# Two-layer hybrid of four token mixers on one core: the scheduler's priority of weight splits and of the instructions that empty projection banks raised in the mixer stage

## The chip, the cores and the metric

The kernel runs on one core of one Trainium2 chip. The metric is device time in microseconds (us) of one execution. The core has a matmul engine, TensorE (PE in the profile; its weight loads are PEld), ScalarE (ACT), VectorE (DVE), GpSimd (POOL) and SyncE (SP), which here only issues transfers. PE runs at one of two clock levels, 1.2 or 2.4 GHz; the profile gives the granted clock as a share of 2.4 GHz.

## The reference, cut to what matters

256 tokens of width 1024 pass through two layers. In each, one in-projection feeds four mixers of 256 columns (hgrn2, gla, rwkv7, retention), an output projection and a layer norm follow, and then a feed-forward block: dense in layer 0, eight experts with two chosen per token in layer 1.

```python
for l in range(DEPTH):
    p = jnp.einsum('btd,dc->btc', h, w_in[l]).astype(F32)
    pa, pb, pc, pd = _split(p, MIXER_COLS)
    ya = _hgrn2_mixer(pa, lb_all[l], hgrn_norm_g[l])
    yb = _gla_mixer(pb, gla_gate_w2[l], gla_gate_b[l], gla_norm_g[l])
    yc, v_first = _rwkv7_mixer(pc, v_first, v_mix, ...)
    yd = _retnet_mixer(pd, positions, log_gamma)
    mix = jnp.einsum('btc,cd->btd', jnp.concatenate([ya, yb, yc, yd], axis=-1), w_out[l])
    h = _layer_norm(DN_ALPHA * h + mix, ln1_g[l], ln1_b[l])
    f = _swiglu(...) if l % 2 == 0 else _moe(...)
    h = _layer_norm(DN_ALPHA * h + f, ln2_g[l], ln2_b[l])
```

## The kernel before, in words

Every large product is computed to nearly f32 accuracy from two reduced-precision halves of each operand: `mm3` issues three matmuls per 128-row block of the contraction, high by high, high by low, low by high. The activations are split once per layer (tile XT). Weights are streamed: `load` has SP fetch a block of 256 columns (1 MB) into one of three `raw` buffers, and `pieces` splits it in three pieces of 3, 3 and 2 row blocks: ACT copies a piece to the high half (tile wH, `self.act`, L133), DVE subtracts that from raw for the low half (wL, `self.tt`, L136). There are three wH and three wL buffers. What `pieces` issues stands in `with self.tc.high_priority(self.hp)`; `self.hp` is HP in the mixers and 0 elsewhere. HP is a number by which an instruction counts as that much earlier in the program when the scheduler picks, engine by engine, the next instruction to write down. The order so written is what each engine runs, in that order.

The in-projection of a layer has fifteen full groups of 256 columns, 48 matmuls each, and a narrow one of 24: 744 matmuls. Each full group fills two PSUM banks, `Pws_ps` (weights stationary) or `Pas_ps` (activations stationary), out of a pool `acc` of three. A bank is free for the next group when its result has been read out: for rwkv by `rwkv_columns` (ACT writes rc_sh, DVE rc_x from bank and rc_sh), for queries, keys and values by `put` (ACT, tiles p_q, p_v), for gates by `silu2` (ACT then DVE, p_g), for gla's q and k by `gla_qk`, for hgrn's forget gate by `hgrn_gate` (DVE).

`mixers` runs rwkv first and then retention, hgrn and gla (ORDER = "rhg"). A mixer is a long chain of small steps that goes back and forth between PE, ACT, DVE and POOL. The groups for the later mixers are jobs: `between(n)` puts steps of them between the steps of the running mixer, so PE has in-projection matmuls to run while a chain is on the other engines. They are called fill here. When the fill of a layer is used up, the first blocks of the output projection (`out_proj`, tiles bank_acc and bank_r, 100 matmuls of 512 columns) serve instead: 52 of them (four that add alpha times h, and 48 for the rwkv and retention rows of w_out) need nothing of hgrn and gla; the last 48 wait for those two mixers' results. Their weights are split by the same `pieces`.

Names that come up: rw_rn (norm of rwkv's keys), rw_E (its decays), rw_kk, rw_ka (its keys), rw_AR and rw_BK (operands of its chunk products Prw_pss), rw_OC (its output), rt_o (retention's output), hg_E and Phs_p1p (hgrn's decays and scores), Pga, gs_lfH and gs_lfL, gs_E, Pgs, Ppo (gla's gate, the halves of its log decays, its decays, scores and output), hn_s and hn_rs (the norm of a mixer's output), y_late and Ppy (a mixer's result and its transpose, which feeds the output projection).

```python
            with self.tc.high_priority(self.hp):
...
                    self.split(H, L, raw[:, k0:k0 + m, :], eng)
```

Of the kernel before, what the change touches and what calls it, by code (L numbers as in the profile page):

```python
# [13 lines left out]
AF = mybir.ActivationFunctionType  # L14
OP = mybir.AluOpType
# [4 lines left out]
T = 256  # L20
# [19 lines left out]

ORDER = "rhg"

HP, OUTK = 60, (6, 4, 0, 2)

TAIL, DT = 4, 4

# [78 lines left out]
class Build:  # L125
# [156 lines left out]
    def ws(self, w, parts, ms=(128, 128), first=False):  # L282
        g = self.ws_steps(w, parts, ms, first)
        while True:
            try:
                next(g)
            except StopIteration as x:
                return x.value
# [339 lines left out]
    def mixers(self, l):  # L628
        nc, I, c, p = self.nc, self.I, self.c, self.otp
        W = I["w_in"][l]  # L630
        self.mp, self.side, self.hp = self.rp, "r", HP
        ws = lambda c0: self.ws_steps(W, [(c0, c0 + 256)])
        as_ = lambda c0: self.as_steps(W, [(c0, c0 + 256)])
        self.jobs = []

        def proj(kind):
            return p.tile([128, 2, 256], F32, name="p_" + kind, bufs=PB.get(kind, 1))

        def put(kind, ps, **k):
            dst = proj(kind)  # L640
            for i, x in enumerate(ps):
                self.act(dst[:, i, :], x, **k)
            return dst

        def silu2(kind, ps):

            dst = proj(kind)
            for i, x in enumerate(ps):
                self.act(dst[:, i, :], x, AF.Tanh, scale=0.5)
                self.stt(dst[:, i, :], dst[:, i, :], 1.0, x, OP.add, OP.mult)  # L650
            return dst
        def gla_qk(ps):
            gqk = proj("q")
            self.act(gqk[:, 0, :], ps[0], scale=float(32 ** -0.5))
            self.act(gqk[:, 1, :], ps[1])
            return gqk[:, 0:1, :], gqk[:, 1:2, :]
        q_, v_, g_ = (lambda ps: put("q", ps)), (lambda ps: put("v", ps)), (lambda ps: silu2("g", ps))
        J = {"h": lambda: [self.job(as_(256), lambda ps: self.hgrn_gate(ps)), self.job(ws(0), lambda ps: silu2("q", ps)),
                           self.job(as_(512), v_), self.job(as_(768), g_)],
             "g": lambda: [self.job(ws(O_GLA), gla_qk), self.job(as_(O_GLA + 256), v_), self.job(as_(O_GLA + 528), g_)],  # L660
             "r": lambda: [self.job(ws(O_RET), q_), self.job(ws(O_RET + 256), q_), self.job(as_(O_RET + 512), v_), self.job(as_(O_RET + 768), g_)]}
        J = {k: J[k]() for k in ORDER}
        glr = p.tile([128, T], F32, name="glr")
        nc.vector.memset(glr[32:64, :], 1.0)
        self.rwkv(l, glr)
        self.mp, self.side = self.otp, "o"
        steps = {"h": lambda f, q, v, g: self.hgrn(l, f, q, v, g),
                 "g": lambda qk, v, g: self.gla(l, glr, qk, v, g),
                 "r": lambda q, k, v, g: self.retnet(l, lambda i: (q, k)[i](), v, g)}
        for k in ORDER:  # L670
            steps[k](*J[k])

    def hgrn_gate(self, px):
        xf = self.otp.tile([128, 2, 256], F32, name="hg_xf")
        for tt, x in enumerate(px):
            self.ts(xf[:, tt, :], x, -44.0, None, OP.max)
        return xf

    def hgrn(self, l, xf, qT, V, G):  # L680
# [273 lines left out]
    def rwkv_columns(self, l, ci, glr):  # L954

        nc, W = self.nc, self.I["w_in"][l]
        c0 = O_RWKV + 256 * ci
        if ci < 4:
            ps, m = self.ws(W, [(c0, c0 + 256)], first=l == 0 and ci == 3), 128
        else:  # L960
            ps, m = self.ws(W, [(c0, c0 + 32), (O_GLA + 512, O_GLA + 528)], (48,)), 32
            nc.vector.tensor_copy(glr[32:48, :], ps[0][32:48, :])
        if ci == 3:
            self.layer_params(l)
        mu = self.pc["mu"]
        n = len(ps)

        sh = self.t2([128, 2, T], n="rc_sh")
        nc.gpsimd.memset(sh[:, :, 0:1], 0.0)
        x = self.t2([128, 2, T], n="rc_x")  # L970
        for j in range(n):
            g = 2 * ci + j
            self.act(sh[0:m, j, 1:T], ps[j][0:m, 0:T - 1], scale=mu[0:m, g:g + 1])
            self.stt(x[0:m, j, :], ps[j][0:m, :], self.om[0:m, g:g + 1], sh[0:m, j, :], OP.mult, OP.add)
        return x

    def rwkv(self, l, glr):
# [706 lines left out]
```

## Time and profile before

| | us |
|---|---|
| median of 3 runs | 1094.89 |
| lowest and highest of them | 1093.45 and 1101.36 |
| profiled execution | 1099.03 |
| its span, first to last instruction | 1097.2 |

The profiled execution is 4.14 us above the median; durations come from it. Times in the rows count from the start of its span. The mixers of layer 0 run to about 213 us, output projection and norm to about 232, the dense block to about 412; the mixers of layer 1 run from about 430 to 633, and the experts from about 660 to the end. In a timeline row stand start, length, engine, line, operation, output <- inputs, operand sizes and count; the bracket gives how long the engine had been idle and what released it. A matmul row's length reaches past the start of the next, since matmuls are pipelined; the distance of starts is what one costs.

### The profile page before, as it was taken

What the parts mean: (1) busy time and instruction counts of PE and PEld (TensorE: products, weight loads), DVE (VectorE), ACT (ScalarE), POOL (GpSimd) and SP (SyncE); (2) the same over time, 40 slices, a digit from 0 to 9 for tenths busy, and PEclk for the clock granted to TensorE, in tenths of its full rate; (3) what the DMA queues carried; (4) which work ended last, traced back from release to release, by engine and by line L of the source; (5) the groups of instructions that cost most, each with busy time, mean ns of one, the idle gap of its engine ahead of it and who ended that gap; (6) DMA issues with size and microseconds to landing.
All of it is one profiled execution on the core that took longest, in us unless ns stands there. A gap on an engine that the chain in (4) does not pass through costs nothing. (4 is left out here: it accounts for less than half of the span.)

```text
span 1097.2 us, 16969 instructions
## 1 busy us (share of the span) xinstructions
PE 1040.8 (95%) x6635; PEld 905.2 (83%) x6635; DVE 789.8 (72%) x1174; ACT 616.8 (56%) x872; POOL 60.5 (6%) x89
## 2 busy tenths in 40 slices
PE   7799989999999999899989989999999999999994
PEld 6788878789999788788877668888888888878883
DVE  4585674565556356675675578998999899989986
ACT  4634264435555342633264536787788678777862
POOL 2000021100000002000011210000000000010001
PEclk9899987999999999899988998999999999999997
DMA  9344144326666454244142095998899889979942
GB/s 299 99 119 128 57 154 155 116 78 192 193 192 228 157 192 156 87 115 131 65 164 78 12 366 191 359 381 302 313 348 362 307 306 364 357 269 328 365 179 80
DMA packets 142161, 228.83 MB, mean 209 GB/s; under 512 B 17604, under 2 KB 89848, under 8 KB 142072
## 3 DMA queue, kind: packets, MB, share of 16 engines
q1 hardware_dynamic: 135104, 219.76, 59.0%
q10 hardware_dynamic: 6968, 7.90, 2.2%
q8 instruction: 54, 0.88, 0.3%
q14 instruction: 35, 0.29, 0.1%
HBM read 224.50 MB, written 3.15 MB: 207 GB/s over the span
## 5 line engine op out<-in xcount | busy, mean ns | idle before, releaser
L136 DVE TENSOR_TENSOR wL<-raw,wH 128x1024 fp32r<-128x1024 f32 (+2 forms) x480 | 504.1, 1064 | 159.2 <-ACT wH L133 152.3
L133 ACT ACTIVATE wH<-raw 128x1024 fp32r<-128x1024 f32 (+2 forms) x481 | 441.9, 927 | 271.0 <-PE Pws_ps L146 95.8
L146 PE MATMUL Pws_ps<-XT,wH 128*128 128x256 f32 (+1 forms) x1248 | 233.2, 287 | 9.1 <-DVE rc_x L143 8.3
L146 PE MATMUL Pms_ps<-wH,e_X 128*128 128x512 f32 (+1 forms) x768 | 227.3, 374 | 0.0
L146 PEld LDWEIGHTS Pws_ps<-XT,wH 128*128 128x128 f32 (+1 forms) x1248 | 195.7, 191 | 12.8 <-DVE rc_x L143 9.2
L146 PE MATMUL Pws_ps<-XT,wL 128*128 128x256 f32 (+1 forms) x624 | 177.9, 286 | 0.0
L146 PEld LDWEIGHTS Pms_ps<-wH,e_X 128*128 128x128 f32 x768 | 142.3, 188 | 20.8
L146 PE MATMUL Pms_ps<-wL,e_X 128*128 128x512 f32 (+1 forms) x384 | 144.7, 377 | 1.0 <-DVE wL L136 1.0
L146 PEld LDWEIGHTS Pws_ps<-XT,wL 128*128 128x128 f32 (+1 forms) x624 | 119.3, 191 | 0.8 <-issue 0.3
L146 PE MATMUL bank_dn<-wH,e_aT 128*128 128x512 f32 x352 | 112.3, 396 | 0.6 <-DVE e_X L136 0.6
L146 PE MATMUL Pas_ps<-wH,XT 128*128 128x256 f32 x448 | 97.3, 305 | 4.6 <-ACT p_v L133 3.2
L146 PEld LDWEIGHTS Pas_ps<-wH,XT 128*128 128x128 f32 x448 | 76.8, 203 | 10.2 <-ACT p_v L133 4.5
L146 PEld LDWEIGHTS Pms_ps<-wL,e_X 128*128 128x128 f32 x384 | 72.2, 188 | 12.7 <-DVE wL L136 2.3
L146 PEld LDWEIGHTS bank_dn<-wH,e_aT 128*128 128x128 f32 x352 | 66.0, 188 | 16.7 <-DVE e_X L136 1.7
L146 PE MATMUL bank_dn<-wL,e_aT 128*128 128x512 f32 x176 | 69.4, 395 | 0.0
L146 PE MATMUL Pas_ps<-wL,XT 128*128 128x256 f32 x224 | 68.2, 305 | 0.5 <-DVE wL L136 0.5
L146 PEld LDWEIGHTS Pas_ps<-wL,XT 128*128 128x128 f32 x224 | 45.4, 203 | 3.1 <-DVE wL L136 1.8
L146 PEld LDWEIGHTS bank_dn<-wL,e_aT 128*128 128x128 f32 x176 | 33.1, 188 | 7.4
L146 PE MATMUL bank_acc<-wH,ffn_a 128*128 128x512 f32 x88 | 33.5, 394 | 0.0
L146 PE MATMUL bank_r<-wH,ffn_a 128*128 128x512 f32 x88 | 33.3, 392 | 0.0
L146 PE MATMUL bank_acc<-wH,YT 128*128 128x512 f32 x64 | 24.5, 416 | 1.2 <-ACT YT L133 1.2
L133 ACT ACT_TABLE_LOAD x19 | 24.4, 1283 | 1.6 <-PEq L1671 1.2
(386 smaller groups left out, 1223.8 us busy)
## 6 DMA issues: line engine op xcount, KB each, us to landing
raw<-in_moe_w_down SPq DMA_DIRECT2D x40, 1024.0 KB
raw<-in_moe_w_gate SPq DMA_DIRECT2D x32, 1024.0 KB
raw<-in_moe_w_up SPq DMA_DIRECT2D x32, 1024.0 KB
raw<-in_w_in SPq DMA_DIRECT2D x29, 1024.0 KB
raw<-in_moe_w_gate SPq DMA_DIRECT2D x16, 768.0 KB
raw<-in_moe_w_up SPq DMA_DIRECT2D x16, 768.0 KB
raw<-in_ffn_w_gate SPq DMA_DIRECT2D x11, 1024.0 KB
raw<-in_ffn_w_up SPq DMA_DIRECT2D x11, 1024.0 KB
```

The source lines that it names most:

```text
L133: return self.nc.scalar.activation(out=out, in_=in_, func=func, **k)
L136: return (eng or self.nc.vector).tensor_tensor(out=out, in0=a, in1=b, op=op)
L146: return self.nc.tensor.matmul(out=out, lhsT=lhsT, rhs=rhs, start=start, stop=stop)
```

## The change

HP goes from 60 to 400, so that the splits of streamed weights in the mixer stage count as 400 places earlier instead of 60. And five places that empty the banks of the in-projections, `put`, `silu2`, `gla_qk`, `hgrn_gate` and the loop of `rwkv_columns`, are put under the same priority, where they had none. No instruction is added or removed and none changes its operands. What changes is the order in which ACT, DVE, PE and SP run theirs; POOL's order is the same.

```diff
@@ -40,7 +40,7 @@
-HP, OUTK = 60, (6, 4, 0, 2)
+HP, OUTK = 400, (6, 4, 0, 2)
@@ -638,21 +638,24 @@
         def put(kind, ps, **k):
             dst = proj(kind)
-            for i, x in enumerate(ps):
-                self.act(dst[:, i, :], x, **k)
+            with self.tc.high_priority(HP):
+                for i, x in enumerate(ps):
+                    self.act(dst[:, i, :], x, **k)
             return dst
...
         def silu2(kind, ps):
             dst = proj(kind)
-            for i, x in enumerate(ps):
-                self.act(dst[:, i, :], x, AF.Tanh, scale=0.5)
-                self.stt(dst[:, i, :], dst[:, i, :], 1.0, x, OP.add, OP.mult)
+            with self.tc.high_priority(HP):
+                for i, x in enumerate(ps):
+                    self.act(dst[:, i, :], x, AF.Tanh, scale=0.5)
+                    self.stt(dst[:, i, :], dst[:, i, :], 1.0, x, OP.add, OP.mult)
             return dst
         def gla_qk(ps):
             gqk = proj("q")
-            self.act(gqk[:, 0, :], ps[0], scale=float(32 ** -0.5))
-            self.act(gqk[:, 1, :], ps[1])
+            with self.tc.high_priority(HP):
+                self.act(gqk[:, 0, :], ps[0], scale=float(32 ** -0.5))
+                self.act(gqk[:, 1, :], ps[1])
             return gqk[:, 0:1, :], gqk[:, 1:2, :]
@@ -673,8 +676,9 @@
     def hgrn_gate(self, px):
         xf = self.otp.tile([128, 2, 256], F32, name="hg_xf")
-        for tt, x in enumerate(px):
-            self.ts(xf[:, tt, :], x, -44.0, None, OP.max)
+        with self.tc.high_priority(HP):
+            for tt, x in enumerate(px):
+                self.ts(xf[:, tt, :], x, -44.0, None, OP.max)
         return xf
@@ -968,10 +972,11 @@
         x = self.t2([128, 2, T], n="rc_x")
-        for j in range(n):
-            g = 2 * ci + j
-            self.act(sh[0:m, j, 1:T], ps[j][0:m, 0:T - 1], scale=mu[0:m, g:g + 1])
-            self.stt(x[0:m, j, :], ps[j][0:m, :], self.om[0:m, g:g + 1], sh[0:m, j, :], OP.mult, OP.add)
+        with self.tc.high_priority(HP):
+            for j in range(n):
+                g = 2 * ci + j
+                self.act(sh[0:m, j, 1:T], ps[j][0:m, 0:T - 1], scale=mu[0:m, g:g + 1])
+                self.stt(x[0:m, j, :], ps[j][0:m, :], self.om[0:m, g:g + 1], sh[0:m, j, :], OP.mult, OP.add)
         return x
```

What that does to the order shows in three places. The first is ACT in layer 0, at the end of rwkv's key norm, where the two banks Pws_ps_416 and 417 (rwkv's receptance, read by rc_sh) and 495 and 496 (retention's queries, read by p_q) are to be emptied. Before:

```order
L133 ACTIVATE rw_rn<-rw_rn 128x512
L133 ACT_TABLE_LOAD
L133 ACTIVATE rw_rn<-rw_rn,rw_b_381 128x512
L133 ACTIVATE rw_E<-Prw_ps_393 128x2x256
L133 ACTIVATE rw_E<-Prw_ps_393 128x256
L133 ACTIVATE rw_E<-Prw_ps_400 128x2x256
L133 ACTIVATE rw_E<-Prw_ps_400 128x256
L133 ACTIVATE rc_sh<-Pws_ps_416,pcol 128x255
L133 ACTIVATE rw_A<-rw_A,psmall 128x256 x2
L133 ACTIVATE rw_AR<-rw_AR 64x8x64
L133 ACTIVATE rw_BK<-rw_BK 64x8x64
```

After:

```order
L133 ACTIVATE rw_rn<-rw_rn 128x512
L133 ACTIVATE p_q<-Pws_ps_495 128x256
L133 ACT_TABLE_LOAD
L133 ACTIVATE rw_rn<-rw_rn,rw_b_381 128x512
L133 ACTIVATE rw_E<-Prw_ps_393 128x2x256
L133 ACTIVATE rw_E<-Prw_ps_393 128x256
L133 ACTIVATE wH<-raw 128x768
L133 ACTIVATE rc_sh<-Pws_ps_416,pcol 128x255
L133 ACTIVATE rc_sh<-Pws_ps_417,pcol 128x255
```

The eviction of bank 495 has moved from behind everything shown to a place ahead of the table load, rc_sh ahead of half of rw_E, and a split stands between.

The second is DVE at the same place, where rc_x is the last reader of bank 416. Before:

```order
L143 SCALAR_TENSOR_TENSOR rw_kk<-rc_x,psmall,rw_rn 128x256 x2
L143 SCALAR_TENSOR_TENSOR rw_ka<-rw_A,rw_kk 128x512
L136 TENSOR_TENSOR rw_AR<-rw_kk,rw_E 128x8x64
L143 SCALAR_TENSOR_TENSOR rw_BK<-rw_ka,rw_E 128x8x64
L143 SCALAR_TENSOR_TENSOR rc_x<-Pws_ps_416,psmall,rc_sh 128x256
L136 TENSOR_TENSOR rc_x<-rc_x,rw_A 128x512
```

After:

```order
L143 SCALAR_TENSOR_TENSOR rw_kk<-rc_x,psmall,rw_rn 128x256 x2
L143 SCALAR_TENSOR_TENSOR rw_ka<-rw_A,rw_kk 128x512
L136 TENSOR_TENSOR wL<-raw,wH 128x768
L143 SCALAR_TENSOR_TENSOR rc_x<-Pws_ps_416,psmall,rc_sh 128x256
L143 SCALAR_TENSOR_TENSOR rc_x<-Pws_ps_417,psmall,rc_sh 128x256
L136 TENSOR_TENSOR wL<-raw,wH 128x768
L136 TENSOR_TENSOR wL<-raw,wH 128x512
L136 TENSOR_TENSOR rc_x<-rc_x,rw_A 128x512
```

rc_x no longer stands behind rw_AR and rw_BK, which feed rwkv's chunk products, but behind a split's low half; rw_AR and rw_BK come after two more splits.

The third is PE in layer 1, at gla's scores (Pgs) with output-projection matmuls (bank_acc, bank_r) among them. Before:

```order
L146 MATMUL bank_r<-wH,YT 128x512
L146 MATMUL bank_acc<-wH,YT 128x512
L146 MATMUL bank_acc<-wL,YT 128x512
L146 MATMUL Pgs_ps_6222<-gs_E 128x256
L146 MATMUL Pgs_ps_6222<-gs_E 128x128
L146 MATMUL Pgs_ps_6233<-gs_E 128x256
L146 MATMUL Pgs_ps_6233<-gs_E 128x128
L146 MATMUL Pgs_ps_6244<-gs_E 128x256
L146 MATMUL Pgs_ps_6244<-gs_E 128x128
L146 MATMUL bank_acc<-wH,YT 128x512
L146 MATMUL bank_r<-wH,YT 128x512
L146 MATMUL bank_r<-wL,YT 128x512
```

After:

```order
L146 MATMUL bank_r<-wL,YT 128x512
L146 MATMUL bank_r<-wH,YT 128x512
L146 MATMUL Pgs_ps_6205<-c_hlR,gs_lfH 128x128
L146 MATMUL Pgs_ps_6205<-c_hlR,gs_lfL 128x128
L146 MATMUL Pgs_ps_6205<-c_hlR,gs_lfH 128x128
L146 MATMUL Pgs_ps_6205<-c_hlR,gs_lfL 128x128
L146 MATMUL Pgs_ps_6222<-gs_E 128x256
L146 MATMUL Pgs_ps_6222<-gs_E 128x128
L146 MATMUL Pgs_ps_6233<-gs_E 128x256
```

Before, the matmul groups of the output projection stand up to Pgs_ps_6222 and between it and Pgs_ps_6259; now all of those that need nothing of hgrn and gla are ahead of Pgs_ps_6205, and nothing stands between the two steps of gla.

## Rows read from the trace of the kernel before

**Rows 1.** Page, part 1: busy time of each engine, share of the span.
```profile
PE 1040.8 (95%) x6635; PEld 905.2 (83%) x6635; DVE 789.8 (72%) x1174; ACT 616.8 (56%) x872; POOL 60.5 (6%) x89
```

**Rows 2.** Busy time by window: us, PE, PEld, DVE, ACT, POOL, granted clock, DMA share, GB/s.
```profile
42.30:49.10 6.80, 6.41 (x34) 6.18 (x35) 4.27 (x7) 3.56 (x6) 0.00 (x0) 0.55 0.01 4
76.50:79.90 3.40, 3.40 (x32) 3.15 (x28) 2.63 (x6) 0.32 (x1) 0.00 (x0) 0.62 0.28 87
138.80:150.00 11.20, 9.66 (x97) 9.03 (x97) 9.38 (x19) 8.47 (x16) 2.95 (x4) 1.00 0.53 170
243.00:351.00 108.00, 108.00 (x923) 108.00 (x922) 64.45 (x100) 58.99 (x100) 0.00 (x0) 1.00 0.61 192
554.30:561.10 6.80, 6.80 (x59) 6.68 (x58) 4.02 (x8) 2.16 (x4) 0.00 (x0) 0.55 0.39 113
574.00:633.10 59.10, 52.13 (x286) 42.14 (x284) 31.41 (x62) 28.26 (x61) 12.19 (x17) 0.88 0.18 57
595.30:608.90 13.60, 13.60 (x50) 10.70 (x49) 3.52 (x8) 6.17 (x15) 4.27 (x4) 0.53 0.16 64
```

**Rows 3.** Timeline of PE where it waited over 0.9 us: start, us, line, instruction, [idle before <- releaser].
```profile
42.69 0.80 PE L146 MATMUL Pws_ps<-XT,wH 128*128 128x256 f32 x2 [4.52 <-DVE rc_x L143]
...
65.47 0.39 PE L146 MATMUL Pas_ps<-wH,XT 128*128 128x256 f32 x1 [0.93 <-ACT p_q L133]
...
73.94 0.38 PE L146 MATMUL Pas_ps<-wH,XT 128*128 128x256 f32 x1 [1.74 <-ACT p_v L133]
...
138.85 1.15 PE L146 MATMUL Prw_ps<-ident,rw_OC 64*64 64x64 f32 x32 [1.36 <-DVE rw_OC L136]
...
143.60 0.63 PE L149 MATMUL Ppy_ps<-ident,rt_o 128*128 128x128 f32 x4 [1.49 <-DVE rt_o L143]
...
456.05 0.80 PE L146 MATMUL Pws_ps<-XT,wH 128*128 128x256 f32 x2 [3.81 <-DVE rc_x L143]
...
554.10 1.97 PE L146 MATMUL Prw_ps<-ident,rw_OC 64*64 64x64 f32 x32 [4.45 <-DVE rw_OC L136]
...
633.08 0.66 PE L149 MATMUL Ppy_ps<-ident,y_late 128*128 128x128 f32 x4 [2.27 <-DVE y_late L136]
```

**Rows 4.** Timeline of ACT around the first long wait of layer 0.
```profile
39.30 1.61 ACT L133 ACTIVATE rw_E<-Prw_ps 128x512 f32<-128x512 f32 x4
40.79 0.49 ACT L133 ACTIVATE rc_sh<-Pws_ps,pcol 128x255 f32<-128x255 f32 x1
```

**Rows 5.** Timeline of DVE at the same place.
```profile
40.96 0.68 DVE L136 TENSOR_TENSOR rw_AR<-rw_kk,rw_E 128x512 f32<-128x512 f32 x1
...
42.16 0.47 DVE L143 SCALAR_TENSOR_TENSOR rc_x<-Pws_ps,psmall,rc_sh 128x256 f32<-128x256 f32 x1
```

**Rows 6.** Groups by line and shape, 27 to 243 us: busy us, mean ns | idle before.
```profile
L136 DVE TENSOR_TENSOR wL<-raw,wH 128x768 fp32r<-128x768 f32 x29 | 27.6, 952 | 12.4 <-ACT wH L133 12.3
L133 ACT ACTIVATE wH<-raw 128x768 fp32r<-128x768 f32 x30 | 25.1, 842 | 31.4 <-PE Pws_ps L146 19.8 <-PE Pas_ps L146 9.4 <-issue 2.2
```

**Rows 7.** Timeline of ACT before the gla scores of layer 1.
```profile
616.52 1.28 ACT L133 ACT_TABLE_LOAD   x1
617.82 0.91 ACT L133 ACTIVATE gs_E<-gs_d 128x128 f32<-128x128 f32 x4
```

**Rows 8.** Timeline of DVE behind gla's last matmul, layer 1.
```profile
626.51 0.69 DVE L610 TENSOR_REDUCE hn_s<-hn_sq 128x8 f32<-128x512 f32 x1 [3.46 <-ACT hn_sq L133]
```

**Rows 9.** Timeline of POOL at the same place.
```profile
627.63 1.27 POOL L136 TENSOR_TENSOR p_g<-p_g,gn_ng 128x512 f32<-128x512 f32 x1
628.86 1.66 POOL L136 TENSOR_TENSOR hn_rs<-rs_ve,mhalf 128x8 f32<-128x8 f32 x1
```

**Rows 10.** Timeline of PE in layer 0: output-projection matmuls under gla's norm.
```profile
202.23 0.48 PE L146 MATMUL bank_acc<-wH,YT 128*128 128x512 f32 x1
...
211.42 0.40 PE L146 MATMUL bank_r<-wH,YT 128*128 128x512 f32 x1
...
213.21 0.63 PE L149 MATMUL Ppy_ps<-ident,y_late 128*128 128x128 f32 x4
```

## The prediction

> **What bounds the kernel now.** I read four views. First the page: PE is busy 95% of the span [rows 1], so the time is PE's work, its waits and the time it spends at the lower clock. The change adds and removes no work, so only waits and clock can move. Second, busy time by window: where weights stream and nothing else happens, PE is 100% busy at clock 1.00 (923 matmuls in 108.00 us, 0.117 us each [rows 2]). The dense block and the experts look like this throughout; there is nothing to win there, and the change does not reach them. What is left are the two mixer stages, to 213 us and from 430 to 633.
>
> Third, PE's timeline in those stages. It has three waits of about 4 us: 4.52 us for rc_x in layer 0, 3.81 for the same in layer 1, 4.45 for rw_OC in layer 1; and small ones of 0.93, 1.74, 1.36, 1.49 and 2.27 us [rows 3]. After each long wait the clock falls: behind the first and the third, windows of 6.80 us were granted 0.55, the lower of the two levels for nearly all of them [rows 2], and behind the second it reads alike. Work done at half rate for 6.8 us takes 3.4 us more than at full rate. So a long wait costs about 4.3 + 3.4 us. Some falls follow no wait: 595.30 to 608.90 was granted 0.53 with PE busy throughout, during hgrn's 64-row matmuls [rows 2]; those the change does not touch.
>
> Fourth, ACT and DVE at the first long wait. PE waits for bank 416. Its readers are rc_sh on ACT, which starts at 40.79 behind rw_E's 1.61 us, and rc_x on DVE, which starts at 42.16 behind rw_AR (0.68 us) and rw_BK [rows 4, 5]. The bank was full long before; its eviction stood in the queue behind rwkv's own steps.
>
> **The change part by part.** All sums are against the profiled execution, 1099.03 us, and carried to the median of 1094.89, 4.14 lower.
>
> *Layer 0, the wait for rc_x.* In the new order the eviction of bank 495 comes ahead of rw_rn's last table load, so half a group, 24 more matmuls or 24 x 0.117 = 2.8 us, can run before PE needs bank 416. That bank itself comes free no sooner: on ACT a split of 0.84 us [rows 6] takes the place of the half of rw_E that now comes later (0.8 us of 1.61), and on DVE rc_x has a low half of 0.95 us [rows 6] ahead of it in place of two steps of 0.68. So the wait shrinks from 4.52 to about 1.8, and a short one for 495 appears, which I put at 0.6 (p_q is issued the moment rw_rn's step ends, between zero and one such step). Gain 4.5 - 1.8 - 0.6 = 2.1 us, bounds 0 and 4.5. Whether the clock still falls: after 1.74 us of waiting it fell in this trace (76.50 to 79.90 was granted 0.62), after 1.36 and 1.49 it did not (138.80 to 150.00 at 1.00) [rows 2, 3]. A coin toss; I take half of 3.4, so 1.7. What is late next: rw_AR and rw_BK come two splits later, and rwkv's chunk products with them by about 2 us, but 52 more in-projection matmuls stand in front of those products in the new PE order, so PE is busy meanwhile.
>
> *Layer 0, 54 to 80 us.* Now banks 665 and 666 are held longer (their rc_sh comes later, behind gate evictions and a table load), and six half groups pass through the one bank left, each waiting for its own eviction. Before, two waits, 0.93 + 1.74 = 2.7 us [rows 3]. After, I count five: two as long as an eviction takes to come up (0.4 each), three that have a split (0.84) or a table load (1.28 [rows 7]) in front and a DVE step behind (1.2, 1.3 and 2.3). Together 5.6: a loss of 2.9. Bounds: a gain of 2.7 if evictions follow at once, and a loss of 8 if each of six banks waits for a whole split (0.84 + 0.95).
>
> *Layer 0, 138 to 144 us.* By the order, 40 more fill matmuls (4.7 us) are done before PE reaches rw_OC and 13 before rt_o; the chains slip by some 2 us, so 1.36 + 1.49 = 2.85 [rows 3] goes. Bounds 0 and 2.85.
>
> *Layer 0, the end.* Fill used earlier is missing later. From 202.23 on, 40 output-projection matmuls, (211.42 - 202.23)/39 = 0.236 us each, covered 9.4 of the 11.0 us from gla's last product to its second transpose at 213.21 [rows 10]. In the new order 31 are left: 9 x 0.236 = 2.1 us of cover gone, and PE itself is late. Loss 2.1, bounds 0 and 4.
>
> Layer 0 in sum: 2.1 + 1.7 - 2.9 + 2.85 - 2.1 = 1.65 us gained.
>
> *Layer 1, the wait for rc_x.* Same code, same reordering: 2.1/4.52 of 3.81 is 1.8, and 1.7 for the clock: 3.5. Bounds 0 and 7.2.
>
> *Layer 1, the wait for rw_OC.* 93 more fill matmuls (663 instead of 570) are done before PE needs rw_OC. That is 10.9 us of work against a wait of 4.45, so the wait goes even if rwkv's chain slips by 5 us, and with it the fall of clock: 4.45 + 3.4 = 7.85. Bounds 3.4 and 7.85.
>
> *Layer 1, hgrn and gla.* Here it is paid back. Before, 57 fill matmuls were still to come when hgrn started; now none. From 574.00 to 633.10 PE was busy 52.13 of 59.10 us, idle 7.0 [rows 2]. Take out 57 x 0.117 = 6.7 us of work, and if hgrn's and gla's chains are as long as before the stretch does not shrink: 13.7 us idle. The order says where: out-projection matmuls now run dry before gla's scores, so that from Pgs_6205 to Pgs_6222 PE stands for table load 1.28, exponentials 0.91 [rows 7] and the steps around them, some 3.3 us; and behind gla's last product the norm chain, from hn_s at 626.51 over p_g 1.27 and hn_rs 1.66 on POOL to the transpose at 633.08 [rows 3, 8, 9], keeps 12 matmuls (2.8 us) of cover. I take 13: a loss of 6. Bounds: 2 (chains get shorter where splits no longer stand in them) and 13 (splits of w_out, 1 us and more each, put ahead of the chains' steps).
>
> Layer 1 in sum: 3.5 + 7.85 - 6 = 5.35. Both layers: 7.0 us gained, 1099.03 - 7.0 = 1092.0 on the profile's scale, **1088 on the median's**.
>
> *A rule weighed.* The trace has waits of 0.93 and 1.74 us on banks between 65 and 74 us, and a fall of clock after the second, from 76.5 [rows 2, 3]. The Trainium skill, TensorE: Matmul & The Clock Gate, section "A second HAM failure mode: psum-queue depth-cycling", says that a matmul stream which idles briefly and often as it cycles through PSUM banks loses clock again and again. By the trace, one fall; by that rule more, since the change makes five such waits in place of two, and the result is the third rival below.
>
> **The rivals.**
>
> *Nearly all of it is won (A).* If PE's 24 matmuls of lead keep the clock up at rc_x in both layers, evictions in 54 to 80 follow at once, and hgrn's chain runs faster without fill in its way: layer 0 gives 2.1 + 3.4 + 0 + 2.85 - 1 = 7.35, layer 1 1.8 + 3.4 + 7.85 - 2 = 11: 1094.9 - 18.4 = 1076.5. For it: the three long waits and their clocks are 12.8 + 10.2 = 23 us, by far the largest item. Against it: bank 416 is not freed sooner.
>
> *Slower: layer 1 is left without fill (B).* With no fill from hgrn's start, idle in 574 to 633 grows by 13 instead of 6, and the waits between gla's steps let the clock fall twice more, 6.8: 19.8 lost. Against it stand the gains as forecast, 1.65 in layer 0 and 11.35 in layer 1: 6.8 lost in sum, 1101.7. If the falls behind rwkv's waits stay as well (6.8 of these gains), it is 13.6: 1108.5. I take the middle, 1105. It decides from the point where the idle added between Phg and the last Ppy passes 13 us, that is when it is 20 us in all. For it: idle was already 7 there with fill to run. Against it: the chains themselves have less on ACT and DVE to wait for.
>
> *The clock follows the bank waits (C).* One more fall of 6.8 us in 54 to 80 and in the like stretch of layer 1, 3.4 lost in each: 1095.
>
> *It does not do what it says (D).* The queue still holds rw_rn's table loads ahead of rc_sh, so the waits only move and the clock falls as before: layer 0 loses 2.9 and 2.1 and gains 2.85, and of layer 1 rw_OC's 7.85 - 6 stays: 1095.2.
>
> **How the numbers follow.** About what a measurement of this kernel can tell from no change is 1%, 11 us: 1084 to 1106. Forecast 0.47 with 1081 to 1095 of its own, A 0.22, B 0.16, C 0.08, D 0.07. Faster by over 1%: three quarters of A and a third of the forecast, 0.32. Slower: most of B and little else, 0.14. Within: 0.54. The range takes in A's value with some excess and B's end at 1106: 1073 to 1106.
>
> **What would show it.** Right: PE's wait at 42.7 of some 2 us, none over 1 us at rw_OC in both layers, PE idle of 12 to 14 us between hgrn's start and gla's last transpose in layer 1 with the largest pieces at Pgs_6222 and Ppy. Wrong: rc_x's wait still above 4 us (D); clock below 0.8 in a window between 54 and 80 in which it was 1.00 (C); that last stretch longer than 65 us (B) or shorter than 55 (A).

## The result and the profile after

Twenty runs of the changed kernel gave a median of 1103.67 us (1097.61 to 1116.60), twenty of the kernel before 1099.60 (1092.65 to 1104.37). The ratio is 1.0051, with a 95% interval of 1.0031 to 1.0072: slower by half a per cent. All ratios in this text are of fast runs alone, so this one is not the quotient of the two medians (1.0036). The forecast was 1088, seven us faster; the sign was wrong. The three runs shown ahead of the prediction lay low: later medians of before are 1097.4 to 1099.6, so 2.5 to 4.7 us of the miss are that scale.

The profiled execution took 1111.14 us, with a span of 1109.0 and a mean granted clock of 0.957, against 1099.03, 1097.2 and 0.965 before. The page's busy times after, to be set beside [rows 1]:

```profile
PE 1056.5 (95%) x6635; PEld 914.3 (82%) x6635; DVE 790.3 (71%) x1174; ACT 616.9 (56%) x872; POOL 62.0 (6%) x89
```

The instructions are the same, 6635 on PE, and DVE and ACT are busy as long as before. PE is busy 15.7 us longer with the same matmuls. That is what a lower clock looks like: the work takes longer, and nobody waits. (Part of it has another source, shown at the end: matmuls that ran two at a time now run one at a time.)

Next the waits. These are PE's longest in the mixers after, from its timeline, with two short ones that take the place of a long one:

```profile
40.05 0.50 PE L146 MATMUL Pws_ps<-XT,wH 128*128 128x256 f32 x2 [0.47 <-ACT p_q L133]
...
44.99 0.50 PE L146 MATMUL Pws_ps<-XT,wH 128*128 128x256 f32 x2 [1.43 <-DVE rc_x L143]
...
61.90 0.38 PE L146 MATMUL Pas_ps<-wH,XT 128*128 128x256 f32 x1 [0.47 <-ACT p_q L133]
...
69.19 0.39 PE L146 MATMUL Pas_ps<-wH,XT 128*128 128x256 f32 x1 [0.55 <-ACT p_v L133]
...
74.31 0.38 PE L146 MATMUL Pas_ps<-wH,XT 128*128 128x256 f32 x1 [1.98 <-DVE p_g L143]
...
150.81 0.39 PE L146 MATMUL Prw_ps<-ident,rw_OC 64*64 64x64 f32 x6 [1.54 <-DVE rw_OC L136]
...
190.47 1.59 PE L146 MATMUL bank_acc<-h,alphaI 128*128 128x512 f32 x2 [2.19 <-DVE p_g L143]
...
459.05 0.50 PE L146 MATMUL Pws_ps<-XT,wH 128*128 128x256 f32 x2 [2.04 <-ACT p_q L133]
...
576.19 1.00 PE L146 MATMUL Prw_ps<-ident,rw_OC 64*64 64x64 f32 x27 [1.44 <-DVE rw_OC L136]
...
629.65 1.67 PE L146 MATMUL Pgs_ps<-gs_E 32*128 32x256 f32 x12 [4.84 <-DVE gs_E L136]
```

Beside [rows 3] the change did what it says. The wait for rc_x in layer 0 went from 4.52 to 0.47 + 1.43, in layer 1 from 3.81 to 2.04 (for p_q now), and rw_OC's in layer 1 from 4.45 to 1.44. In their place stand 2.19 us at 190 and 4.84 us at gla's scores. All idle time of PE added up over its timeline from 6 to 260 us is 14.8 before and 15.4 after, and from 400 to 680 us 20.2 before and 16.9 after. [rows 3] is not complete: the trace of before has three more waits over 0.9 us in the mixers, 1.32 at 28.57, 1.42 at 579.34 and 1.20 at 628.71.

Then the clock, in windows of the kernel after: behind rc_x in layer 0; in rwkv's steps from Prw_bkt (a transpose by 64x64 matmuls) to Prw_gate, layer 0; behind p_q, then the same steps of rwkv, in layer 1; behind rw_OC; and hgrn and gla of layer 1:

```profile
46.40:53.20 6.80, 6.80 (x61) 6.55 (x60) 6.77 (x11) 4.69 (x8) 0.23 (x1) 1.00 0.55 171
76.30:79.70 3.40, 3.40 (x19) 3.18 (x18) 2.54 (x6) 1.69 (x6) 0.00 (x0) 0.70 0.00 0
86.00:100.00 14.00, 14.00 (x74) 12.43 (x72) 3.78 (x7) 5.57 (x10) 0.00 (x0) 0.63 0.33 81
459.05:465.85 6.80, 6.80 (x57) 6.63 (x59) 6.70 (x11) 5.79 (x10) 0.00 (x0) 1.00 0.22 55
510.00:530.00 20.00, 20.00 (x103) 16.19 (x103) 4.38 (x10) 4.71 (x9) 0.00 (x0) 0.66 0.06 19
576.20:583.00 6.80, 6.80 (x78) 6.59 (x79) 6.80 (x11) 3.28 (x6) 0.00 (x0) 1.00 0.72 281
587.30:646.40 59.10, 51.65 (x244) 40.43 (x243) 29.23 (x60) 26.35 (x57) 11.80 (x17) 0.80 0.14 43
```

Behind the three long waits the clock was 0.55 or read alike [rows 2]; behind the shorter ones it is now 1.00. So that part of the forecast came true. But rwkv's steps are granted 0.63 and 0.66 with PE busy in every microsecond. In the kernel before the same steps were at full clock:

```profile
82.00:96.00 14.00, 14.00 (x113) 12.38 (x112) 5.90 (x12) 8.80 (x16) 0.00 (x0) 1.00 0.52 141
496.50:516.50 20.00, 20.00 (x238) 17.57 (x236) 9.99 (x17) 8.39 (x15) 0.00 (x0) 1.00 0.48 156
```

The counts in the first brackets (113 matmuls then, 74 now; 238 then, 103 now) are of windows of one length, not of the same steps: at the lower clock fewer steps fit in. Count between the same steps instead, from rwkv's first Prw_pss on rw_UV to its first Prw_gate. Two things differ there. The first is fill: 70 in-projection matmuls stood there in layer 0 and 34 in layer 1; the changed order has 29 and 7, because banks that are emptied earlier let the fill run earlier. The second is the order of the small matmuls. Those of Prw_pss and Prw_bkt have 64 rows each and belong to one or the other half of PE's 128 rows; the kernel's loop takes the halves in turns. Where they do take turns, the trace shows two matmuls under way at a time. In before's order at most ten of one half come in a row in Prw_pss and eight in Prw_bkt, then the halves alternate; in the changed order it is twelve or fourteen in Prw_pss, and in Prw_bkt all 16 of one half, 2 of fill, and the 16 of the other. So layer 1 takes 10.58 us from Prw_pss to Prw_gate (510.45 to 521.03) with 7 of fill, and took 9.32 (497.05 to 506.37) with 34.

Lastly the mixers' end in layer 1. 59.10 us of it had 6.97 idle, at 0.88 [rows 2]; a window as long after has 7.45 idle, at 0.80, and 42 matmuls fewer. The same steps, from hgrn's first Phg to the last Ppy, took 59.47 us (573.61 to 633.08) and take 58.19 (587.35 to 645.54).

To hold many runs against each other I split each run's time in two: the loss, (1 - granted clock) x span, and the rest. The loss counts idle time at the lower clock too. Means of runs taken together, with a standard error: the changed kernel, run again, has a loss of 40.0 (1.3) and a rest of 1063.2 (0.5); before has 34.9 (0.8) and 1062.7 (0.4). So 5.1 (1.5) of the 5.5 us between their means lie in the loss, and 0.5 (0.6) in the rest.

### The profile page after: what moved, and what is told of

The parts are those of the page before. It is cut to its first block, busy times and chain, and to the rows that moved or that the text cites. A ratio compares the mean times of both kernels' runs of the same rounds, so it can differ in the third digit from the quotient of the medians.

```text
span 1109.0 us, 16968 instructions
## 1 busy us (share of the span) xinstructions
PE 1056.5 (95%) x6635; PEld 914.3 (82%) x6635; DVE 790.3 (71%) x1174; ACT 616.9 (56%) x872; POOL 62.0 (6%) x89
## 5 line engine op out<-in xcount | busy, mean ns | idle before, releaser
L146 PE MATMUL Pws_ps<-XT,wH 128*128 128x256 f32 (+1 forms) x1248 | 229.6, 284 | 5.7 <-ACT p_q L133 2.5
L146 PEld LDWEIGHTS Pws_ps<-XT,wH 128*128 128x128 f32 (+1 forms) x1248 | 192.2, 188 | 10.1 <-ACT p_q L133 3.4
L146 PEld LDWEIGHTS Pws_ps<-XT,wL 128*128 128x128 f32 (+1 forms) x624 | 117.0, 188 | 1.5 <-DVE wL L136 0.7
L146 PE MATMUL bank_acc<-wH,YT 128*128 128x512 f32 x64 | 27.8, 470 | 0.8 <-ACT YT L133 0.8
L146 PE MATMUL bank_r<-wH,YT 128*128 128x512 f32 x64 | 26.4, 446 | 0.0
```

The lines of the kernel that those rows point to most:

```text
L146: return self.nc.tensor.matmul(out=out, lhsT=lhsT, rhs=rhs, start=start, stop=stop)
```

## The experiments

The expectations set several theories against each other: that the time went to the clock; that rwkv's chain is delayed by evictions and splits now ahead of its own steps (V); and that no part does anything, since the clock's falls differ from run to run (L). E, C, P and M are said where they come up. HPS below gives the priority by layer, in the order splits, rwkv_columns, put, silu2, gla_qk, hgrn_gate; the changed kernel is six times 400 in both, the kernel before (60, 0, 0, 0, 0, 0). Changes of loss and rest, in us, are against runs of before taken together with each; their standard errors are 1.3 to 2.3 and 0.6 to 1.1 us, 3.4 and 1.4 for x2.

| run | ratio, 95% | loss | rest |
|---|---|---|---|
| x1_splits | 1.0231, 1.0205 to 1.0257 | +16.2 | +8.3 |
| x2_evict | 1.0203, 1.0166 to 1.0241 | +17.5 | +3.6 |
| x3_layer0 | 1.0033, 1.0014 to 1.0053 | +0.4 | +2.4 |
| x4_layer1 | 1.0030, 1.0008 to 1.0052 | +4.9 | -0.5 |
| x5_rc | 1.0047, 1.0018 to 1.0076 | +5.5 | +0.2 |
| x6_dummies_after | 1.0094, 1.0066 to 1.0121 | -2.3 | +12.2 |
| x7_dummies_before | 1.0048, 1.0023 to 1.0073 | -4.7 | +9.3 |
| x8_all150 | 1.0116, 1.0090 to 1.0142 | +3.2 | +8.3 |
| x9_same_order | 1.0014, 0.9996 to 1.0033 | +0.1 | +0.9 |
| x10_dummies_rcx | 0.9963, 0.9938 to 0.9989 | -6.6 | +2.0 |
| x11_dummies_half | 0.9996, 0.9969 to 1.0023 | -1.8 | +2.1 |
| x12_changed_again | 1.0052, 1.0024 to 1.0080 | +5.1 | +0.5 |
| x13_gs_dummies | 1.0052, 1.0021 to 1.0084 | +2.6 | +2.8 |
| x14_rcx_again | 0.9933, 0.9908 to 0.9958 | -9.8 | +1.9 |

**One half of the change alone.** x1 raises the splits only, x2 the evictions only.

```diff
-HPS = ((400, 400, 400, 400, 400, 400), (400, 400, 400, 400, 400, 400))
+HPS = ((400, 0, 0, 0, 0, 0), (400, 0, 0, 0, 0, 0))
...
+HPS = ((60, 400, 400, 400, 400, 400), (60, 400, 400, 400, 400, 400))
```

> Only the splits get the higher number (60 to 400); the evictions have no priority, as before. By its order this kernel has 736 of 744 fill matmuls behind it when hgrn starts in layer 1 (before 687, changed kernel 738), so it spends fill as early as the changed kernel, without the earlier evictions. Theory E (the loss comes from fill being spent early, so that rwkv's and gla's small steps run bare): at least as slow as the changed kernel, ratio to before 1.005 to 1.015, PE waits of 3 us or more before gla's scores of layer 1, and the waits for rc_x near 4 us still there. Theory V (the loss comes from evictions standing ahead of rwkv's chain on ACT and DVE): ratio 0.997 to 1.002, as before. Theory L (no part does anything, the clock's falls differ from run to run): every one of these four kernels within 0.997 and 1.003.

> Only the evictions get priority 400; the splits stay at 60. By its order 669 fill matmuls are behind it when hgrn starts in layer 1, fewer than before (687), and 16 of 52 free output-projection matmuls at gla's scores (before 24, changed kernel 52). Theory E: faster than before, ratio 0.990 to 0.997, with the waits for rc_x shorter than 4 us or gone and PE idle between hgrn's start and gla's last transpose in layer 1 at most 7 us as before. Theory V: slower, 1.003 to 1.008. Theory L: 0.997 to 1.003.

Each half is 2% slower, more than any theory said, and the whole only 0.5%: the halves need each other. x1 shows how an order can go wrong where the change itself does nothing. First PE, then ACT, in x1's timeline behind the mixers of layer 1:

```profile
655.57 0.80 PE L148 MATMUL bank_acc<-wH,YT 128*128 128x512 f32 x1 [5.77 <-ACT YT L135]
```

```profile
647.57 0.48 ACTq L1408 DMA_DIRECT2D e_rt<-in_moe_router  x1
...
654.77 0.26 ACT L135 ACTIVATE e_rHL<-e_rt 128x64 fp32r<-128x64 f32 x1 [13.09 <-DMA e_rt<-in_moe_router]
654.93 0.58 ACT L135 ACTIVATE YT<-Ppy_ps 128x512 fp32r<-128x512 f32 x1
```

ACT runs in order. The split of the router's weights, e_rHL, stands ahead of the copy YT that PE waits for, and its own load was issued at 647.57 and landed at 654.77. In the kernel before e_rHL stands ahead of that copy too, but its load was issued at 628.88, ahead of the last Ppy, and e_rHL ran at 631.26; in x1 the issue comes behind the last Ppy (646.44). That wait alone is 5.8 us of x1's 8.3 in the rest. The same wait is 3.57 us in x2's profile, 4.76 in x7's and 5.18 in x8's, and none of 0.3 us stands at that place in before's; these are the four runs whose rest is over 3 us longer, x6 with its added matmuls aside. The 16 us of x1's loss are not pinned to one place.

**One layer alone.**

```diff
+HPS = ((400, 400, 400, 400, 400, 400), (60, 0, 0, 0, 0, 0))
...
+HPS = ((60, 0, 0, 0, 0, 0), (400, 400, 400, 400, 400, 400))
```

> The whole change in layer 0, the kernel before in layer 1. In layer 0 fill lasts nearly to the end in both orders (Pga at 722 against 678 of 744). Theory E: small, 0.998 to 1.003. Theory V: half of the change's loss, 1.002 to 1.004, since rwkv's chain is the same in both layers. Theory L: 0.997 to 1.003. The two layers' ratios less one should add up to the changed kernel's 0.005.

> The kernel before in layer 0, the whole change in layer 1, where fill is used up when hgrn starts. Theory E: most of the change's loss stands here, 1.003 to 1.008, with the wait for gs_E before gla's scores (4.8 us in the changed kernel). Theory V: half of it, 1.002 to 1.004. Theory L: 0.997 to 1.003.

Each layer costs 0.3%, and the two add up to the whole within their intervals; ratios so near each other tell the theories poorly apart. The layers do not cost it in the same way: layer 0 in the rest, 2.4 (0.7), layer 1 in the clock, 4.9 (1.5). Of layer 0's 2.4, 0.9 lies outside the span, ahead of the first or behind the last instruction: x3's runs are 2.7 us longer than their spans, before's 1.8. x4's window over rwkv's steps of layer 1 reads as the changed kernel's, to the matmul:

```profile
508.90:528.90 20.00, 20.00 (x104) 16.19 (x103) 4.50 (x10) 4.59 (x9) 0.00 (x0) 0.66 0.05 17
```

**Smaller doses.** x5 raises rwkv_columns only, x8 everything, but to 150.

```diff
+HPS = ((60, 400, 0, 0, 0, 0), (60, 400, 0, 0, 0, 0))
...
+HPS = ((150, 150, 150, 150, 150, 150), (150, 150, 150, 150, 150, 150))
```

> The kernel before, with priority 400 for the two instructions that empty rwkv's banks (rc_sh, rc_x) and for nothing else. The order keeps before's fill almost to the matmul (189 to 192 fill matmuls ahead of rwkv's first chunk products, the same counts from there on). Theory C (what costs is the clock: it falls where rwkv's small matmuls run with no fill between them, and behind a wait of 4 us): the waits for rc_x shrink or go, no new falls appear in rwkv, ratio to before 0.993 to 0.998. Theory V (an eviction ahead of rwkv's chain delays the chain): 1.002 to 1.006.

> The changed kernel with 150 in place of 400, for splits and evictions alike. Its order spends fill between before and the changed kernel: 354 fill matmuls ahead of rwkv's transposed values in layer 0 (337 before, 384 changed), 697 when hgrn starts in layer 1 (687, 738). Theory C: fall of clock in rwkv's small matmuls in some of the layers, ratio 0.997 to 1.004, below the changed kernel's. Theory V: 1.003 to 1.006, since rwkv's chain has evictions ahead of it just the same.

x5 still has a wait of 3.91 us for rc_x, hardly a changed rest, and a loss 5.5 us higher; its 1.0047 lies in the range of theory V, but by the clock and not by a delay, and C's range failed. In its profile the clock falls in rwkv's steps of layer 0, where its order has about as much fill as before's (72 against 70). So thin fill is not needed for a fall. Nor is it enough. x1 and x2 have nearly the same fill in rwkv's steps of layer 1, 7 and 10 matmuls, but in x1 the halves of Prw_bkt run one after the other and in x2 they take turns. x1, then x2, each with Prw_bkt and the window of the steps:

```profile
509.66 2.00 PE L148 MATMUL Prw_bkt<-ident,rw_BK 64*128 64x64 f32 x16
...
512.02 3.14 PE L148 MATMUL Prw_bkt<-ident,rw_BK 64*128 64x64 f32 x16
...
506.20:519.80 13.60, 13.60 (x81) 10.45 (x80) 2.24 (x5) 3.54 (x7) 0.00 (x0) 0.74 0.24 76
```

```profile
505.82 2.50 PE L148 MATMUL Prw_bkt<-ident,rw_BK 64*128 64x64 f32 x32
...
502.37:511.40 9.03, 9.03 (x84) 7.42 (x83) 2.32 (x3) 2.97 (x5) 0.00 (x0) 1.00 0.38 118
```

All sixteen profiles, two layers each, sort the same way. In thirteen of these 32 stretches the clock falls, and in each of them one half had run alone for longer before the fall than in any stretch without one, as the times say: the 32 of Prw_pss take 2.87 to 3.76 us, or, in x1's layer 1, 16 of Prw_bkt take 1.93. The fill of these thirteen is 7, 29 or 58 to 73 matmuls. In the nineteen without a fall the 32 of Prw_pss take 2.65 us and the 32 of Prw_bkt 2.42 to 2.72 (2.95 and 2.94 in x6 below, which has other matmuls between); their fill is 10, 19, 22, 30 to 39 or 70. So the halves sort the stretches and the count of fill does not. No run changes the halves alone, so that they are the cause is not shown.

x8 missed both of its ranges. It lies between x1 and the change and shows that 400 is not simply too much; 5.18 us of it are the wait for YT.

**Is the order all there is?** x9 is the kernel before, written with the HPS table; x12 the changed one, written so.

> The kernel before, written through the same switches as the other experiments: every engine's order is that of before. It measures what two kernels with one order differ by. All theories: ratio 0.998 to 1.002, and (1 - granted clock) x span as before's, 35 us.

> The changed kernel once more, on the same chip as the three others and with a second profile. Ratio 1.003 to 1.007. By the theory that the change's loss is clock (theory M's consequence for it): (1 - granted clock) x span 39 to 43 us against before's 35, and the rest of the time within 1.5 us of before's. By theory V (evictions delay rwkv's chain): the rest is longer by 4 us or more.

x9 is 1.0014 with no change of loss, x12 repeats 1.0052, both as expected. Orders reproduce, so theory L falls: some orders cost 2%, the old one written anew costs nothing, and falls come back in the same places. In rwkv's steps of layer 1 each of the four profiles of the changed order there (the first, x4, x12, x13) shows one, between 504 and 530 us; of the profiles of before, x3, x9, x10 and x14, none does. The same four show another that starts 20 to 24 us ahead of it, in the first at 494.80 to 501.60 (granted 0.50), behind a wait of 0.73 us at 492.12; the other five have none there. x12's row, to be set beside 510.00:530.00 above:

```profile
506.40:526.40 20.00, 20.00 (x104) 16.20 (x103) 4.41 (x10) 4.66 (x9) 0.00 (x0) 0.66 0.09 28
```

V, as the expectation put it, falls by the rest: if the chain were delayed, PE would wait, and the rest would be 4 us longer or more. It isn't, in x4 and x12.

**Putting work back into rwkv's steps.** x6 is the changed kernel with matmuls on a constant between the four steps of Prw_pss and of Prw_bkt and ahead of Prw_gate, in both layers, written into columns that are overwritten later.

```diff
+            if ch < 3:
+                self.warm(pss[0][:, (ch + 1) * 128:512], 4, w)
...
+        self.warm(pg, 4, w)
```

> [...] Theory C: with these between the small matmuls the clock stays at 1.00 in rwkv from Prw_pss to Prw_XY in both layers, where the changed kernel lost 5.1 and 6.8 us by it; 3.8 us per layer are added and some 5 to 6 saved, ratio 0.998 to 1.004 against the changed kernel's 1.005. If small matmuls are not the cause, the clock falls all the same and the ratio is 1.010 to 1.013.

```profile
503.79:520.43 16.64, 16.64 (x120) 13.03 (x120) 3.01 (x6) 4.16 (x8) 0.00 (x0) 1.00 0.18 60
82.40:99.35 16.95, 16.92 (x124) 13.18 (x123) 5.34 (x10) 4.72 (x10) 0.00 (x0) 1.00 0.43 122
```

Both stretches, from the first Prw_pss to Prw_bonus, are now granted 1.00, where the changed kernel had 0.66 and 0.63, and the change of loss goes from +5.1 (x12) to -2.3. So what stands in these steps decides whether the clock falls there. Which part of it does is not shown, for x6 changes three things: it adds wide matmuls; it makes the halves take turns, 24 of each 32 now running in eights of both halves in 0.6 us; and its order has 22 and 19 of fill there in place of 29 and 7. As a cure it fails: the ratio is 1.0094, worse than the 0.998 to 1.004 that theory C gave, though the clock did what C said. In layer 1 the stretch takes 16.64 us, against 15.18 at the low clock (510.45 to 525.63). 12 more of fill make up 1.4 us of that; the added matmuls cost the rest of what the clock gives back.

**Filling the new wait.** x13 is the changed kernel with 20 such matmuls ahead of gla's scores in layer 1.

```diff
+        self.warm(self.bank("o", "Pwarm"), (0, 20)[l], w)
         d = self.t2([128, 256], n="gs_d")
```

> The changed kernel with 20 matmuls of 128x512 on a constant, ahead of gla's scores in layer 1, where the changed kernel's PE stood 4.84 us for gs_E; nothing else is touched. 20 x 0.227 = 4.5 us of work in 4.84 us of idle time. If the low clock behind that wait (628 to 646, 8.5 us lost in the first profile, 10.2 in the second) is part of what makes the change slower: loss of clock about 8 us less than the changed kernel's 41, and 1.0052 becomes 0.998 to 1.000. If the low clock only stands beside it and the waits are what costs: no gain, 1.005 or a little more.

The wait of 4.84 us is down to 0.8, and the time is the same. The windows show why:

```profile
600.00:618.00 18.00, 18.00 (x68) 14.64 (x67) 6.08 (x14) 6.78 (x16) 4.27 (x4) 0.53 0.01 3
...
628.00:640.00 12.00, 11.23 (x45) 9.51 (x45) 3.36 (x7) 2.29 (x6) 3.54 (x4) 0.57 0.30 66
```

The clock is low from 600 on, in hgrn's small matmuls, ahead of the place, and again behind it. The wait for gs_E was not what kept it down. Of the two outcomes expected, 0.998 to 1.000 failed, and no gain is what came.

**Filling the old waits.** These take the kernel before and put matmuls on a constant ahead of its waits: x7 in rc_x's (16 in layer 0, 14 in layer 1) and in rw_OC's of layer 1 (16); x10 in rc_x's alone, x11 half as many; x14 is x10 again.

```diff
+        self.warm(self.bank("o", "Pwarm"), (16, 14)[l], w)
         BK = p.tile([128, 8, 3, 64], F32, name="rw_BK")
...
         ps = self.mx("Prw_ps14")
+        self.warm(ps, (0, 16)[l], self.last)
```

The second of these lines is in x7 only.

> The kernel before with matmuls that compute nothing used ahead of its three long waits: 16 (3.8 us) ahead of layer 0's wait for rc_x, 14 ahead of layer 1's, 16 ahead of layer 1's wait for rw_OC. They take up time in which PE would idle. Theory C: the three falls behind these waits (3.4 us each in the profile of before) go, ratio 0.991 to 0.997. If the falls come of something else than the wait, 0.999 to 1.003.

> The kernel before with 16 matmuls that compute nothing used ahead of layer 0's wait for rc_x and 14 ahead of layer 1's, and none ahead of rw_OC. Theory P (the wait itself is cheap to fill, and the fall of clock behind it costs 3.4 us): both falls go, ratio 0.992 to 0.997. If clock falls only move elsewhere when one is avoided (theory M), (1 - granted clock) x span stays within 2 us of before's 35 and the ratio is 0.998 to 1.002.

> The same with half as many, 8 and 7: waits of some 2.6 and 2.2 us are left, about the size that the changed kernel leaves (1.4 to 2.0). Theory P: falls behind waits of this size go as well, 0.993 to 0.998. If a wait of 2 us is enough for a fall: 0.998 to 1.002. Theory M: 0.998 to 1.002.

> The kernel before with 16 and 14 such matmuls in its two waits for rc_x, run a second time. If the gain of the first run is real: 0.994 to 0.999, with a loss of clock about 6 us under the kernel before's. If it was chance: 1.000.

x10 and x14 are the fastest of all, 0.9963 and 0.9933, with losses 6.6 and 9.8 us under before's. x14's timeline and windows show it:

```profile
35.26 3.80 PE L148 MATMUL Pwarm<-eyeR 128*128 128x512 f32 x16
...
436.74 3.35 PE L148 MATMUL Pwarm<-eyeR 128*128 128x512 f32 x14
...
444.24 0.51 PE L148 MATMUL Pws_ps<-XT,wH 128*128 128x256 f32 x2 [1.33 <-DVE rc_x L145]
```

```profile
40.60:47.40 6.80, 6.80 (x61) 6.29 (x61) 6.73 (x11) 3.77 (x8) 0.00 (x0) 1.00 0.05 13
76.00:90.00 14.00, 14.00 (x111) 12.31 (x110) 6.08 (x12) 8.76 (x16) 0.00 (x0) 1.00 0.59 161
...
484.00:504.00 20.00, 20.00 (x238) 17.66 (x237) 10.04 (x17) 8.28 (x16) 0.00 (x0) 1.00 0.43 138
```

The useless matmuls take the time in which PE stood for rc_x, the wait in layer 0 is gone, the fall behind it is gone, and rwkv's steps keep their order: 238 matmuls in 20 us, at 1.00. In layer 1 a wait of 1.33 us is left. This wins what the change meant to win without moving the fill. Theory P's range held x10; x14 came out better than its range, 0.994 to 0.999. In both the rest is 1.9 or 2.0 us longer, which nothing here explains. Half the number (x11) wins nothing that can be measured: 0.9996, as was expected if the waits that are left (1.36 us in layer 0; 1.25, 0.91 and 1.12 in layer 1) are enough for a fall, and its profile has falls behind the waits of layer 1. x7, with 16 more at rw_OC, has a loss 4.7 us lower too, but 9.3 us more in the rest, and at 1.0048 missed both of its ranges; 4.76 of it are the wait for YT behind the router's split that x1 showed.

## Why the prediction was wrong, and where it was right

The sum had 7.0 us of gain: 6.8 of clock and 0.2 of everything else. Measured on runs side by side, everything else lost 0.5 (0.6), within its error of the forecast, and the clock lost 5.1 (1.5) where 6.8 were to come back. The failed step is the clock: the sum took back the falls behind three waits and put at nothing, without saying so, what the new order does to the clock in rwkv's own steps, where PE does not wait. There the profile after loses 5.2 and 6.8 us. That everything else came out is luck: its terms below missed in both directions and cancelled.

*Layer 0, rc_x.* Forecast 1.8 + 0.6 left, measured 1.43 + 0.47, and the clock stays at 1.00 behind it. Right. The coin toss of 1.7 for the clock came up as the full 3.4.

*54 to 80 us.* Five waits of 5.6 us in sum were forecast, three of 3.0 came (0.47, 0.55, 1.98). The loss of 2.9 was 0.3. The clock fell once behind the last (76.3 to 79.7 was granted 0.70), as before. The Trainium skill's rule on depth-cycling that was weighed there, and rival C with it, did not come true at this place: in 54 to 80 there is no further fall.

*138 to 144.* Forecast gone, but rw_OC still waits 1.54 and a split 0.83 (at 144.74).

*Layer 0, the end.* Loss forecast 2.1; it came, but as 2.19 us at 190.47, for p_g, not as missing cover at the norm.

*Layer 1, rc_x and rw_OC.* Of 3.81 were to go 1.8, and 1.77 went. Of 4.45 all was to go; 1.44 stayed, behind steps of rwkv that had become slower. The falls of clock behind both went, as forecast. What the step left out is that the 93 matmuls of fill that run earlier come in part out of rwkv's own runs of small matmuls, and that these runs come out in another order, half after half. In this stretch the profile after loses 6.8 us, (1 - 0.66) x 20, where before lost nothing. Together with the fall at 86 to 100 in layer 0, (1 - 0.63) x 14 = 5.2, this takes back the 10.2 us of the three falls that went; the fall at 494.80 adds 3.4.

*Layer 1, hgrn and gla.* Idle was to grow from 7.0 to 13; it is 7.45 with the piece at gs_E as forecast (4.84, by my count 3.3). The stretch is 1.3 us shorter, so the working's first half nearly holds: the chains set it. Its second half doesn't. Of the 6.7 us that the missing fill left, 1.3 went, 0.5 are idle, and most of the others went into matmuls at a lower clock, (0.88 - 0.80) x 59.1 = 4.7 us.

Of the rivals, none describes the outcome. B has the sign, but by idle time behind hgrn's start, and that did not come. C has the mechanism, a clock that falls more often, but at the wrong place: it looked at waits on banks, and the falls came where PE never waits. The Trainium skill's rule that lay behind it, and the neighbouring section "HAM oscillation — how this bites in real kernels" of the Trainium skill's TensorE: Matmul & The Clock Gate, both put falls down to PE pausing between groups of matmuls. The trace differs here: 20.00 of 20.00 us busy at 0.66, and no idle time of PE from 493.11 to the fall at 515.3. (The ends of matmuls are modelled, so pauses much shorter than a matmul would not show.) By the rule the removal of waits should help the clock; the measurement decides. My own rows had hinted at it, the fall at 595.30 with PE busy throughout [rows 2], and I set it aside as one "the change does not touch"; a wait of 0.87 us at 591.49, too short for [rows 3], stands ahead of that one.

What stays open: whether it is the halves or something that goes with them that lets the clock fall in rwkv's steps; layer 0's 2.4 us in the rest (x3), of which 0.9 lie outside the span and 0.6 are PE's longer idle time in the profile (halves run one after the other would cost some 1.6 us there at full clock, an estimate from 3.10 against 2.65 us for Prw_pss and twice x1's 1.93 against 2.72 for Prw_bkt); and x1's and x2's high losses, which no run took apart.

## What to carry to other kernels

A priority that moves evictions and splits moves everything that the scheduler places around them. Before trusting the sum over waits, compare in both orders how each run of small matmuls comes out: how many wide matmuls stand in it, and whether its two row halves still take turns. A run that PE executes without a wait can still lose its clock, and here the runs that lost it were those in which one half ran alone. A wait that costs clock behind it can be cheaper to fill with useless work (0.9933 and 0.9963 here) than to remove by reordering (1.0051), when the work takes about as long as the wait; half as much won nothing (0.9996), and added matmuls where PE is busy anyway cost 1.0094.

## What the runs showed of the hardware

Two 64-row matmuls on different halves of PE's rows ran in about the time of one, at either clock level. The kernel after, layer 1, then the kernel before:

```profile
514.12 2.66 PE L146 MATMUL Prw_bkt<-ident,rw_BK 64*128 64x64 f32 x16
...
517.43 3.67 PE L146 MATMUL Prw_bkt<-ident,rw_BK 64*128 64x64 f32 x16
521.03 4.67 PE L146 MATMUL Prw_gate<-rw_SG,rw_g 128*128 128x256 f32 x8
```

```profile
500.43 2.50 PE L146 MATMUL Prw_bkt<-ident,rw_BK 64*128 64x64 f32 x32
```

From start to next start, the second 16 took 3.60 us (517.43 to 521.03, granted 0.50), 0.225 each; before, 32 took 2.43 (500.43 to 502.86, granted 1.00), 0.076 each. That is three times, but only a factor of two of it is the clock. In x1, whose halves run one after the other as in the kernel after, 16 took 1.93 us at 1.00 (509.66 to 511.59), 0.121 each, against 0.225 at 0.50. The other factor is the turns. The starts of single matmuls show it: while one half runs alone they stand 0.112 us apart at 1.00 and 0.213 at 0.50, and while the halves take turns two start every 0.112 us at 1.00 (before, 501.04 to 501.37) and every 0.21 at 0.50 (x5, 90.90 to 91.33). The 8 of Prw_gate took 4.60 at 0.50 and 2.40 in x6 at 1.00, the two times of the clock.

The clock can fall with PE busy: in layer 1 of the kernel after it fell at 515.3, with no idle time of PE in its timeline since 493.11. What PE ran just before the fall were 64-row matmuls of one half alone, which is what the experiments sort by.
